# One decoder kernel: the seven-product up-projection with the queues of four engines in a hand-written order, and its gating moved from POOL to DVE

## The chip, the cores and the metric

The kernel runs on one core of a Trainium2 chip. A core has TensorE (PE, matrix products into the accumulators called PSUM), VectorE (DVE), ScalarE (ACT), GpSimd (POOL) and SyncE (SP, which here only issues DMA transfers). Each engine works through its own queue in order, and waits on semaphores that other engines raise. The metric is the device time of one execution in microseconds (us); the median of several runs is compared.

## What is computed

Two decoder layers over 512 tokens of width 1024 in float32. Each layer has a token mixer (dilated attention heads and mLSTM heads), a cross-attention into 256 memory tokens, and a gated MLP. The change touches the MLP:

```python
def conv_ffn(h, w_up, conv_w, conv_b, w_down):
    u = causal_dwconv(h @ w_up, conv_w, conv_b)      # width 3, along the tokens
    a, g = jnp.split(u, 2, axis=-1)                  # 2816 columns each
    return (jax.nn.gelu(g, approximate=True) * a) @ w_down
```

## The kernel before

Every float32 matrix product is made of three products of two-part operands. `split` makes the parts: ACT casts a tile to its high part (`hi`, line 99), then DVE subtracts that from the tile for the low part (`lo`, line 100). `mm3` then issues hi*hi, hi*lo and lo*hi (line 107).

The up-projection has 22 pairs of column blocks; pair j is one block of 128 linear columns (A) and one of 128 gate columns (G), against 512 tokens. Pairs 0 and 1 go through `feat_halves` as ordinary products. Pairs 2 to 21 go through `up_products`, the phase that the change rewrites. There a pair is taken as a 2 by 2 block product and is made with seven block products instead of eight (Winograd's form of Strassen's algorithm). One product is four `mm3`, so 12 matmuls of 256 columns, and a pair has 84 matmuls. There are 20 pairs in each of two layers, 40 in all.

For pair j the phase needs four kinds of weight operands, each split in high and low:

- `a`: the linear block as loaded (`raw`, line 86)
- `t` and `u`: sums made by POOL out of the two loaded blocks `raw` and `rg` (lines 1069 to 1072, four subtractions of 128x512: the first two make the tile `t12`, operand `t`; the last two make `t34`, operand `u`). Their tiles are named `T`
- `b`: one half of the gate block `rg`, loaded at line 1066

`raw` and `rg` have two buffers each. A buffer of `raw` comes free when POOL's fourth subtraction and the split of that pair have read it; only then can SP issue the load of the pair after next into it. The tile `T` has three buffers.

After the products come the sums in PSUM (ACT copies at lines 1105, 1123 and 1133, DVE additions at lines 1125 and 1134), the convolution of each half (`up_conv`: one ACT pass at line 1022, two DVE passes at line 1024, which read the accumulator), the GELU of the gate half (ACT, line 1027), and the product of both halves (POOL, line 1041), which goes to `down`, the down-projection.

Only PE's queue follows the order in which the code is written. The order of the other four queues is made by a scheduler, with a cost model, from the dependencies. PE takes, for pair j: product 5 of j, product 6 of j, product 4 of j-1, product 1 of j+1, then products 2, 3 and 7 of j.

Of the kernel before, what the change touches and what calls it, by code (L numbers as in the profile page):

```python
# [38 lines left out]
def trunk_kernel(ctx: ExitStack, tc: tile.TileContext, x4, memt, w, gw, gains, mcw, fcw, gb,  # L39
# [970 lines left out]
    def ffn(l, xn, pend, forms):  # L1010
# [8 lines left out]
        def up_conv(j, half, acc):  # L1019
            m = 22 * half + j  # L1020
            u = fp.tile([128, 512], F32, tag=f"u{half}", name=nm("u"), bufs=2)
            ACT.activation(u, acc, AF.Identity, bias=fcw_t[:, m, 3:4], scale=fcw_t[:, m, 2:3])  # L1022
            for q in range(1, 3):
                DVE.scalar_tensor_tensor(u[:, q:], acc[:, :512 - q], fcw_t[:, m, 2 - q:3 - q], u[:, q:],  # L1024
                                         ALU.mult, ALU.add)
            if half:
                ACT.activation(u, u, AF.Gelu_apprx_tanh)
            us[j, half] = u
            if (j, 1 - half) not in us:
                return  # L1030
# [10 lines left out]
            POOL.tensor_tensor(gt, us.pop((j, 0)), us.pop((j, 1)), ALU.mult)  # L1041
            gtiles.append(gt)

# [6 lines left out]
        run(up_products(l, fp, xn, forms, range(2, NF), up_conv))  # L1050
        return es, fp, gtiles

    def up_products(l, fp, xn, forms, pairs, done):


# [4 lines left out]
        left = {1: quarter(0, 0), 2: quarter(1, 0), 4: quarter(1, 1)}  # L1060
        left.update({3: forms.part("s4"), 5: forms.part("s1"), 6: forms.part("s2"), 7: forms.part("s3")})

        def weights(j):
            ra = load_raw(l, U_UP + 2 * j)
            rg = fp.tile([128, 1024], F32, tag="rg", name=nm("rg"), bufs=2)
            SP.dma_start(rg, w[l, U_UP + 2 * j + 1])
            b11, b21, b12, b22 = ra[:, :512], ra[:, 512:], rg[:, :512], rg[:, 512:]
            t12, t34 = forms.flat(), forms.flat()
            POOL.tensor_tensor(t12[:, :512], b12, b11, ALU.subtract)  # L1069
            POOL.tensor_tensor(t12[:, 512:], b22, t12[:, :512], ALU.subtract)  # L1070
            POOL.tensor_tensor(t34[:, :512], b22, b12, ALU.subtract)
            POOL.tensor_tensor(t34[:, 512:], b21, t12[:, 512:], ALU.subtract)  # L1072
            wa = w_split(ra, HALF_OFF)
            wt = w_split(t12, HALF_OFF)
            wb = forms.pool.tile([128, 1120], F32R, tag="b", name=nm("b"))
            wb = wb[:, 96:608], wb[:, 608:1120]
            split(b22, *wb)
            wu = w_split(t34, HALF_OFF)
            return {1: (wa, 0), 2: (wa, 512), 5: (wt, 0), 6: (wt, 512), 3: (wb, 0), 7: (wu, 0), 4: (wu, 512)}

        def product(o, ws, i, start=False):
            (hi, lo), c0 = ws[i]
            for q in range(4):
                c = slice(c0 + 128 * q, c0 + 128 * q + 128)
                rh, rl = left[i](q)
# [4 lines left out]
        hv = (slice(0, 256), slice(256, 512))  # L1090
        sums = [pg() for _ in range(4)]
        ws = {}
        e1s = {}
# [195 lines left out]
```

## Time and profile before

| | us |
|---|---|
| median of 3 runs | 1632.68 |
| lowest, highest | 1632.03, 1633.22 |
| the profiled execution | 1629.01 |
| its span, first to last instruction | 1627.0 |
| PE busy | 1556.9 (96%) |
| DVE busy | 1108.0 (68%) |
| ACT busy | 889.4 (55%) |
| POOL busy | 403.9 (25%) |

Matmuls overlap each other in the records, so a busy PE is not a PE at its peak. POOL works almost only in two stretches, one in each layer: the seven-product phases, from about 463 to 712 us and from about 1260 to 1506 us. The granted PE clock is full over the whole span. A timeline row gives the start in us, the length in us, engine, line, operation, output and inputs, shapes, and in brackets how long the engine stood idle before it and what released it.

### The profile page before, as it was taken

The page shows a single profiled execution, that of the slowest core. Times are in us where ns is not written, and L with a number is a line of the kernel's source. Part 1 is how long each engine was busy: PE and PEld are TensorE (multiplying, and loading weights), DVE is VectorE, ACT ScalarE, POOL GpSimd, SP SyncE. Part 2 cuts the span into 40 slices and gives each one's busy share as a digit, 9 for nine tenths or more (in the row PEclk, how much of TensorE's full clock was granted, in tenths as well). Part 3 has the DMA queues.
Part 4 walks back from the last instruction along what each step waited for, and adds up shares of the span by engine and source line. Part 5 has one row for each costly group of instructions (what it writes and reads, how often), then busy time and mean ns, then how long its engine had stood idle before and what let it go on. Part 6 is the DMA issues. An engine that isn't in the chain of part 4 may idle for free. (4 is left out here: it accounts for less than half of the span.)

```text
span 1627.0 us, 24707 instructions
## 1 busy us (share of the span) xinstructions
PE 1556.9 (96%) x9480; PEld 1372.9 (84%) x9480; DVE 1108.0 (68%) x1804; ACT 889.4 (55%) x1578; POOL 403.9 (25%) x296
## 2 busy tenths in 40 slices
PE   7999999999999998989999999999999899898998
PEld 5788888988899888878887888889888899897886
DVE  5688565756798787773377885656658899799433
ACT  5677564544665555552257775645445556556321
POOL 0000210000156576710010002100001767675000
PEclk9999999999999999999999999999999999999999
DMA  5322344551332222233233222444412222232321
GB/s 175 121 91 75 101 142 147 174 172 46 101 129 79 104 80 104 95 113 116 91 98 105 84 85 91 149 149 156 142 39 81 66 103 91 92 115 87 111 92 64
DMA packets 55432, 173.15 MB, mean 106 GB/s; under 512 B 6801, under 2 KB 9617, under 8 KB 55314
## 3 DMA queue, kind: packets, MB, share of 16 engines
q1 hardware_dynamic: 55314, 171.57, 32.0%
q8 instruction: 74, 1.21, 0.3%
q14 instruction: 44, 0.36, 0.1%
HBM read 165.22 MB, written 6.33 MB: 105 GB/s over the span
## 5 line engine op out<-in xcount | busy, mean ns | idle before, releaser
L100 DVE TENSOR_TENSOR wlo<-raw,whi 128x1024 fp32r<-128x1024 f32 x228 | 291.4, 1279 | 224.2 <-ACT whi L99 221.4
L107 PE MATMUL pg<-B,whi 128*128 128x256 f32 (+1 forms) x1800 | 421.1, 327 | 11.1 <-DVE u L1024 5.9
L99 ACT CAST whi<-raw 128x1024 fp32r<-128x1024 f32 x228 | 239.2, 1050 | 228.1 <-PE pg L107 158.9
L107 PEld LDWEIGHTS pg<-B,whi 128*128 128x128 f32 x1800 | 291.0, 189 | 31.4 <-issue 6.9
L107 PE MATMUL pg<-whi,B 128*128 128x512 f32 x896 | 297.6, 398 | 0.0
L107 PE MATMUL pg<-B,wlo 128*128 128x256 f32 (+1 forms) x896 | 288.6, 322 | 0.0
L107 PE MATMUL pa<-S,whi 128*128 128x256 f32 x960 | 178.2, 286 | 35.7 <-ACT pg L1105 35.5
L226 POOL TENSOR_TENSOR sm<-sm,mhalf 128x1 f32<-128x1 f32 x56 | 34.4, 614 | 688.1 <-DVE sm L351 511.8
L107 PEld LDWEIGHTS pg<-whi,B 128*128 128x128 f32 x896 | 168.5, 188 | 35.1 <-DVE B L100 1.3
L107 PEld LDWEIGHTS pa<-S,whi 128*128 128x128 f32 x960 | 147.7, 189 | 42.3 <-ACT pg L1105 42.1
L107 PEld LDWEIGHTS pg<-B,wlo 128*128 128x128 f32 x896 | 168.8, 188 | 13.7
L107 PE MATMUL pg<-wlo,B 128*128 128x512 f32 x448 | 175.2, 391 | 0.6 <-DVE sm L244 0.6
L1024 DVE SCALAR_TENSOR_TENSOR u<-pg,fcw,u 128x510 f32<-128x510 f32 (+1 forms) x176 | 130.4, 746 | 39.8 <-ACT u L1022 37.0
L100 DVE TENSOR_TENSOR wlo<-T,whi 128x1024 fp32r<-128x1024 f32 x80 | 128.5, 1610 | 33.2 <-ACT whi L99 32.6
L107 PE MATMUL pa<-S,wlo 128*128 128x256 f32 x480 | 135.3, 282 | 0.0
L107 PE MATMUL pg<-whi,S 128*128 128x512 f32 x352 | 116.3, 390 | 3.0 <-DVE u L1024 3.0
L107 PE MATMUL pa<-whi,S 128*128 128x512 f32 x352 | 116.4, 390 | 0.0
L99 ACT CAST whi<-T 128x1024 fp32r<-128x1024 f32 x80 | 84.1, 1052 | 46.5 <-POOL T L1072 27.4
L1069 POOL TENSOR_TENSOR T<-rg,raw 128x512 f32<-128x512 f32 x40 | 71.4, 1785 | 146.5 <-DMA rg<-in_w_dram 114.1
L1022 ACT ACTIVATE u<-pg,fcw 128x512 f32<-128x512 f32 x88 | 68.0, 776 | 71.1 <-DVE pg L1134 71.1
L107 PEld LDWEIGHTS pg<-wlo,B 128*128 128x128 f32 x448 | 84.7, 189 | 15.8 <-DVE wlo L100 1.0
L107 PEld LDWEIGHTS pa<-S,wlo 128*128 128x128 f32 x480 | 90.7, 189 | 0.0
(249 smaller groups left out, 2916.7 us busy)
## 6 DMA issues: line engine op xcount, KB each, us to landing
raw<-in_w_dram SPq DMA_DIRECT2D x228, 512.0 KB, 3.5
rg<-in_w_dram SPq DMA_DIRECT2D x40, 512.0 KB, 4.3
gain<-in_gains_dram SPq DMA_DIRECT2D x11, 512.0 KB, 4.5
raw<-in_memt_dram SPq DMA_DIRECT2D x20, 256.0 KB, 3.0
tb<-tb_d SPq DMA_DIRECT2D x16, 256.0 KB, 3.6
x<-in_x_dram SPq DMA_DIRECT2D x8, 256.0 KB, 5.7
e<-nmu_d SPq DMA_DIRECT2D x8, 256.0 KB, 3.7
dv<-vf SPq DMA_DIRECT2D x8, 256.0 KB, 4.2
```

Of the source, the lines that this page charges most:

```text
L99: ACT.copy(hi, src)
L100: DVE.tensor_sub(lo, src, hi.bitcast(F32))
L107: PE.matmul(o, lhs, rhs, **kw)
L226: POOL.tensor_tensor(r, v, mhalf[:, :1], ALU.pow)
L1022: ACT.activation(u, acc, AF.Identity, bias=fcw_t[:, m, 3:4], scale=fcw_t[:, m, 2:3])
L1024: DVE.scalar_tensor_tensor(u[:, q:], acc[:, :512 - q], fcw_t[:, m, 2 - q:3 - q], u[:, q:], ALU.mult, ALU.add)
L1069: POOL.tensor_tensor(t12[:, :512], b12, b11, ALU.subtract)
```

## The change

In `up_products` the queues of ACT, DVE, POOL and SP now follow the written order too, and the helper functions are taken apart so that this order can be written: `split` becomes `high` (ACT) and `low` (DVE), the loads become `load_a` and `load_g`, POOL's sums `add_up`, and the convolution `conv_first` (ACT) and `conv_rest` (DVE). Product 4 of pair j-1 moves ahead of product 6 of pair j. The gating (`gated`) is a DVE multiplication, no longer a POOL one. In this phase GELU writes its result into the gate's own accumulator in PSUM, and the gating reads it there. The sums that finish pair p = j-1 are issued at the start of step j. Loads of `raw` stand four pairs ahead in the code, loads of `rg` two pairs ahead. Numbers of buffers are unchanged.

```diff
-            POOL.tensor_tensor(gt, us.pop((j, 0)), us.pop((j, 1)), ALU.mult)
+            DVE.tensor_mul(gt, lin, gate)
             gtiles.append(gt)
...
-        run(up_products(l, fp, xn, forms, range(2, NF), up_conv))
+        with tc.manual_schedule(engines={mybir.EngineType.Activation, mybir.EngineType.DVE, mybir.EngineType.Pool,
+                                         mybir.EngineType.SP}):
+            run(up_products(l, fp, xn, forms, us, conv_first, conv_rest, gated))
...
+        def load_a(j):
+            if j < NF:
+                raws[j] = load_raw(l, U_UP + 2 * j)
+        def load_g(j):
+            if j < NF:
+                rgs[j] = fp.tile([128, 1024], F32, tag="rg", name=nm("rg"), bufs=2)
+                SP.dma_start(rgs[j], w[l, U_UP + 2 * j + 1])
...
+        def add_up(j):
+            if j < NF:
...
+                POOL.tensor_tensor(t12[:, :512], b12, b11, ALU.subtract)
+                POOL.tensor_tensor(t12[:, 512:], b22, t12[:, :512], ALU.subtract)
+                POOL.tensor_tensor(t34[:, :512], b22, b12, ALU.subtract)
+                POOL.tensor_tensor(t34[:, 512:], b21, t12[:, 512:], ALU.subtract)
...
+        def high(j, kind):
...
+            ACT.copy(ws[j, kind][0], source(j, kind))
+        def low(j, kind):
+            if j < NF:
+                DVE.tensor_sub(ws[j, kind][1], source(j, kind), ws[j, kind][0].bitcast(F32))
...
+        for j in range(j0, NF + 1):
+            p, real = j - 1, j < NF
+            if p >= j0:
+                A, G = total(p)
+                ACT.copy(A[:, right], e1s[p])
+                DVE.tensor_add(G[:, right], e1s[p], p5s[p])
+            low(j, "b")
+            load_g(j + 2)
+            if p >= j0:
+                conv_first(p, 1, G)
+            if real:
+                e5 = pa()[:, left]
+                yield from product(e5, j, 5, True)
+                p5s[j] = forms.pool.tile([128, 256], F32, tag="p5", name=nm("p5"), bufs=2)
+                ACT.copy(p5s[j], e5)
+            if p >= j0:
+                conv_rest(p, 1, G)
+                yield from product(A[:, right], p, 4)
+            low(j, "u")
+            if p >= j0:
+                conv_first(p, 0, A)
+                ACT.activation(G, us.pop((p, 1)), AF.Gelu_apprx_tanh)
+                conv_rest(p, 0, A)
+            if real:
+                yield from product(e1s[j], j, 6)
+                DVE.tensor_add(total(j)[1][:, left], e1s[j], p5s[j])
+            high(j + 1, "t")
+            low(j + 1, "t")
+            if p >= j0:
+                gated(p, us.pop((p, 0)), G)
+            if j + 1 < NF:
                 yield from first(j + 1)
...
+            high(j + 2, "a")
+            low(j + 2, "a")
+            if j + 1 < NF:
+                ACT.copy(total(j + 1)[0][:, left], e1s[j + 1])
+            add_up(j + 2)
+            load_a(j + 4)
+            if real:
+                yield from product(total(j)[0][:, left], j, 2)
+                high(j + 1, "u")
+                yield from product(total(j)[1][:, left], j, 3)
+                high(j + 1, "b")
+                yield from product(e1s[j], j, 7)
```

The order of ACT's queue before, one pair in the middle of layer 0 (`whi` is a high part from `T` or `raw`, `b` the gate half's, `pg` the sums A and G, `pa` the accumulator of products 1, 6 and 7, `p` the kept product 5, `u` the convolution's result):

```order
L1105 COPY pg_4934<-pa_6050 128x256
L99 CAST b_5998<-rg_5982 128x512
L1133 COPY pg_4932<-pa_5923 128x256
L1022 ACTIVATE u_6102<-pg_4933,fcw_4652 128x512
L1123 COPY p_1203_6145<-pa_6132 128x256
L99 CAST whi_6121<-T_6111 128x1024
L1027 ACTIVATE u_6102<-u_6102 128x512
L99 CAST whi_6128<-T_6112 128x1024
L1022 ACTIVATE u_6172<-pg_4932,fcw_4652 128x512
L99 CAST whi_6244<-raw_6234 128x1024
```

ACT's queue now, the same stretch of the phase:

```order
L1112 CAST whi_6046<-T_5942 128x1024
L1112 CAST whi_6064<-raw_5820 128x1024
L1191 COPY pg_4936<-pa_6051 128x256
L1112 CAST whi_6089<-T_5943 128x1024
L1112 CAST b_6104<-rg_5866 128x512
L1160 COPY pg_4934<-pa_5924 128x256
L1022 ACTIVATE u_6123<-pg_4935,fcw_4652 128x512
L1170 COPY p_1201_6138<-pa_6125 128x256
L1022 ACTIVATE u_6155<-pg_4934,fcw_4652 128x512
L1177 ACTIVATE pg_4935<-u_6123 128x512
```

The same instructions are there; the cast of the second `T` (operand `u`) now stands directly ahead of the cast of `b` and the copy that finishes A, where it stood after GELU. DVE's queue before, in the same place (`wlo` is a low part):

```order
L1134 TENSOR_TENSOR pg_4933<-pa_5923,p_1187_6018 128x256
L1024 SCALAR_TENSOR_TENSOR u_6102<-pg_4933,fcw_4652,u_6102 128x511
L1024 SCALAR_TENSOR_TENSOR u_6102<-pg_4933,fcw_4652,u_6102 128x510
L1125 TENSOR_TENSOR pg_4935<-pa_6050,p_1203_6145 128x256
L100 TENSOR_TENSOR wlo_6122<-T_6111,whi_6121 128x1024
L100 TENSOR_TENSOR wlo_6129<-T_6112,whi_6128 128x1024
L1024 SCALAR_TENSOR_TENSOR u_6172<-pg_4932,fcw_4652,u_6172 128x511
L1024 SCALAR_TENSOR_TENSOR u_6172<-pg_4932,fcw_4652,u_6172 128x510
L100 TENSOR_TENSOR wlo_6245<-raw_6234,whi_6244 128x1024
L100 TENSOR_TENSOR b_6125<-rg_6109,b_6125 128x512
```

DVE's queue now:

```order
L1161 TENSOR_TENSOR pg_4935<-pa_5924,p_1185_6011 128x256
L1116 TENSOR_TENSOR b_6104<-rg_5866,b_6104 128x512
L1027 SCALAR_TENSOR_TENSOR u_6123<-pg_4935,fcw_4652,u_6123 128x511
L1027 SCALAR_TENSOR_TENSOR u_6123<-pg_4935,fcw_4652,u_6123 128x510
L1116 TENSOR_TENSOR wlo_6090<-T_5943,whi_6089 128x1024
L1027 SCALAR_TENSOR_TENSOR u_6155<-pg_4934,fcw_4652,u_6155 128x511
L1027 SCALAR_TENSOR_TENSOR u_6155<-pg_4934,fcw_4652,u_6155 128x510
L1181 TENSOR_TENSOR pg_4937<-pa_6051,p_1201_6138 128x256
L1116 TENSOR_TENSOR wlo_6174<-T_6069,whi_6173 128x1024
L1041 TENSOR_TENSOR B_5922<-u_6155,pg_4935 128x512
L1116 TENSOR_TENSOR wlo_6192<-raw_5948,whi_6191 128x1024
```

The low part of the second `T` moved between the two convolutions, the low part of `b` from the end to the second place, and the gating (line 1041) came in as the eleventh instruction. SP's queue before, loads of `raw` (line 86) and `rg` (line 1066) in the middle of the phase:

```order
L1066 DMA rg_5854<-in_w_dram 128x1024
L86 DMA raw_6107<-in_w_dram 128x1024
L1066 DMA rg_5982<-in_w_dram 128x1024
L86 DMA raw_6234<-in_w_dram 128x1024
L1066 DMA rg_6109<-in_w_dram 128x1024
```

SP's queue now (`raw_5820` and `rg_5994` are the blocks of one pair):

```order
L1087 DMA rg_5866<-in_w_dram 128x1024
L86 DMA raw_5948<-in_w_dram 128x1024
L1087 DMA rg_5994<-in_w_dram 128x1024
L86 DMA raw_6075<-in_w_dram 128x1024
L1087 DMA rg_6121<-in_w_dram 128x1024
```

In both, `raw` of the next pair stands ahead of `rg` of this pair, one by one.

## Rows read from the trace of the kernel before

**Rows 1.** Windows, layer 1's phase: length, busy PE, PEld, DVE, ACT, POOL, clock.
```profile
1276.00:1488.00 212.00, 193.35 (x1586) 189.68 (x1586) 182.19 (x187) 119.91 (x187) 153.07 (x92) 1.00 0.26 93
```
**Rows 2.** Timeline of PE, first matmuls of two products that follow each other.
```profile
696.45 0.41 PE L107 MATMUL pg<-B,whi 128*128 128x256 f32 x2
...
697.89 0.41 PE L107 MATMUL pg<-B,whi 128*128 128x256 f32 x2
```
**Rows 3.** Waits of the whole run: who, for whom, us in total, times, longest.
```profile
POOL T L1069 <- DMA rg<-in_w_dram: 114.1, 33, 5.4
...
PE pa L107 <- ACT pg L1105: 35.5, 29, 2.9
...
ACT whi L99 <- POOL T L1072: 27.4, 28, 2.8
```
**Rows 4.** Timeline of POOL, one pair of layer 1 and the next one's start.
```profile
1397.79 1.82 POOL L1069 TENSOR_TENSOR T<-rg,raw 128x512 f32<-128x512 f32 x1 [3.61 <-DMA rg<-in_w_dram]
1399.68 1.31 POOL L1070 TENSOR_TENSOR T<-rg,T 128x512 f32<-128x512 f32 x1
1400.94 1.32 POOL L1071 TENSOR_TENSOR T<-rg 128x512 f32<-128x512 f32 x1
1402.23 2.26 POOL L1072 TENSOR_TENSOR T<-raw,T 128x512 f32<-128x512 f32 x1
1404.45 1.32 POOL L1041 TENSOR_TENSOR B<-u,u 128x512 f32<-128x512 f32 x1
1409.38 1.81 POOL L1069 TENSOR_TENSOR T<-rg,raw 128x512 f32<-128x512 f32 x1 [3.61 <-DMA rg<-in_w_dram]
```
**Rows 5.** Timeline of SP's queue in the same pair.
```profile
1404.52 0.33 SPq L86 DMA_DIRECT2D raw<-in_w_dram  x1
1404.94 0.39 SPq L1066 DMA_DIRECT2D rg<-in_w_dram  x1
```
**Rows 6.** Timeline of POOL, first subtraction of pairs 2, 5, 21 (layer 0), 5, 21 (layer 1).
```profile
463.36 1.79 POOL L1069 TENSOR_TENSOR T<-rg,raw 128x512 f32<-128x512 f32 x1 [15.99 <-DVE T L304]
...
496.94 1.33 POOL L1069 TENSOR_TENSOR T<-rg,raw 128x512 f32<-128x512 f32 x1 [5.92 <-issue]
...
683.10 2.25 POOL L1069 TENSOR_TENSOR T<-rg,raw 128x512 f32<-128x512 f32 x1 [2.57 <-DMA rg<-in_w_dram]
...
1292.80 2.34 POOL L1069 TENSOR_TENSOR T<-rg,raw 128x512 f32<-128x512 f32 x1 [5.09 <-DMA rg<-in_w_dram]
...
1476.56 2.29 POOL L1069 TENSOR_TENSOR T<-rg,raw 128x512 f32<-128x512 f32 x1 [2.54 <-DMA rg<-in_w_dram]
```
**Rows 7.** Timeline of ACT in the same pair of layer 1.
```profile
1397.06 0.62 ACT L99 CAST b<-rg 128x512 fp32r<-128x512 f32 x1
1397.58 0.38 ACT L1133 COPY pg<-pa 128x256 f32<-128x256 f32 x1
1398.88 0.78 ACT L1022 ACTIVATE u<-pg,fcw 128x512 f32<-128x512 f32 x1 [0.92 <-DVE pg L1134]
...
1401.03 1.05 ACT L99 CAST whi<-T 128x1024 fp32r<-128x1024 f32 x1 [1.11 <-POOL T L1070]
...
1404.53 1.05 ACT L99 CAST whi<-T 128x1024 fp32r<-128x1024 f32 x1 [1.92 <-POOL T L1072]
```
**Rows 8.** Timeline of DVE in the same pair of layer 1.
```profile
1398.36 0.42 DVE L1134 TENSOR_TENSOR pg<-pa,p 128x256 f32<-128x256 f32 x1
1399.69 1.53 DVE L1024 SCALAR_TENSOR_TENSOR u<-pg,fcw,u 128x511 f32<-128x511 f32 x2 [0.91 <-ACT u L1022]
...
1402.11 1.24 DVE L100 TENSOR_TENSOR wlo<-T,whi 128x1024 fp32r<-128x1024 f32 x1 [0.55 <-ACT whi L99]
...
1409.34 0.68 DVE L100 TENSOR_TENSOR b<-rg,b 128x512 fp32r<-128x512 f32 x1
```
**Rows 9.** Groups by line, whole run: a DVE product of an accumulator and an SBUF tile.
```profile
L359 DVE TENSOR_TENSOR hg<-pg,gain 128x512 f32<-128x512 f32 x32 | 21.9, 683 | 0.0
```
**Rows 10.** Timeline of PE, the first matmul of the down-projection in layer 0.
```profile
705.79 0.40 PE L107 MATMUL pa<-whi,S 128*128 128x512 f32 x1
```

More of the change, by code (lines that the diff above doesn't have):

```diff
@@ L1017, in ffn, with conv_first, conv_rest @@
         us = {}
-        def up_conv(j, half, acc):
+        def conv_first(j, half, acc):
             m = 22 * half + j
-            u = fp.tile([128, 512], F32, tag=f"u{half}", name=nm("u"), bufs=2)
+            us[j, half] = u = fp.tile([128, 512], F32, tag=f"u{half}", name=nm("u"), bufs=2)
             ACT.activation(u, acc, AF.Identity, bias=fcw_t[:, m, 3:4], scale=fcw_t[:, m, 2:3])
+        def conv_rest(j, half, acc):
+            m, u = 22 * half + j, us[j, half]
             for q in range(1, 3):
@@ L1025, in up_conv, with gated @@
                                          ALU.mult, ALU.add)
[L1026 to L1030, printed above, removed]
+        def gated(j, lin, gate):
             if j < 16:
@@ L1040, in up_conv @@
                 gt = pp.tile([128, 512], F32, tag="xg", name=nm("gt"), bufs=PACE["xg"])
-            POOL.tensor_tensor(gt, us.pop((j, 0)), us.pop((j, 1)), ALU.mult)
+            DVE.tensor_mul(gt, lin, gate)
             gtiles.append(gt)
+        def up_conv(j, half, acc):
+            conv_first(j, half, acc)
+            conv_rest(j, half, acc)
+            u = us[j, half]
+            if half:
+                ACT.activation(u, u, AF.Gelu_apprx_tanh)
+            if (j, 1 - half) in us:
+                gated(j, us.pop((j, 0)), us.pop((j, 1)))
         def up_done(j, half):
@@ L1058, in quarter @@
             return lambda q: (xn[kh][:, q, c], xn[2 + kh][:, q, c])
[L1060 to L1079, printed above, removed]
@@ L1081, in product @@
-        def product(o, ws, i, start=False):
-            (hi, lo), c0 = ws[i]
+        act = {1: quarter(0, 0), 2: quarter(1, 0), 4: quarter(1, 1)}
+        act.update({3: forms.part("s4"), 5: forms.part("s1"), 6: forms.part("s2"), 7: forms.part("s3")})
+        left, right = slice(0, 256), slice(256, 512)
+        sums = [pg() for _ in range(4)]
+        raws, rgs, ts, ws, e1s, p5s = {}, {}, {}, {}, {}, {}
+        def load_a(j):
+            if j < NF:
+                raws[j] = load_raw(l, U_UP + 2 * j)
@@ L1088, in product @@
                     yield
[L1090 to L1093, printed above, removed]
-        def total(j):
-            i = 2 * (j % 2)
-            return sums[i], sums[i + 1]
         def first(j):
-            e1s[j] = pa()
-            if j - pairs[0] < 2:
+            e1s[j] = pa()[:, left]
+            if j < j0 + 2:
                 for o in total(j):
-                    mm(o, ws[j][1][0][0][:, :128], xn[0][:, 0, :], start=True, stop=True)
-            yield from product(e1s[j][:, hv[0]], ws[j], 1, True)
-            ACT.copy(total(j)[0][:, hv[0]], e1s[j][:, hv[0]])
@@ L1136, in up_products @@
-        yield from last(pairs[-1])
+                    mm(o, ws[j, "a"][0][:, :128], xn[0][:, 0, :], start=True, stop=True)
+            yield from product(e1s[j], j, 1, True)
+        for j in (j0, j0 + 1):
+            load_a(j)
+            load_g(j)
+        add_up(j0)
+        load_a(j0 + 2)
+        for kind in "atu":
+            high(j0, kind)
+            if kind != "u":
+                low(j0, kind)
+        high(j0, "b")
+        yield from first(j0)
+        ACT.copy(total(j0)[0][:, left], e1s[j0])
```

57 lines of the change are left out of this document (28 added, 29 removed).

## The prediction

> **What bounds the kernel now.** I read four views, in this order: engine by stage, then PE's own spacing, then who waits for whom, then the timeline of the engine at the start of that chain. The change touches only the seven-product phase. There POOL, idle elsewhere, is busy 153.07 of 212 us and PE 193.35 [rows 1]: neither is full. One product takes PE 697.89 − 696.45 = 1.44 us [rows 2], so a pair cannot go below 7 × 1.44 = 10.08 us. What it takes is read from POOL, which starts one set of four subtractions per pair: 16 sets from pair 5 to pair 21 last 683.10 − 496.94 = 186.16 us in layer 0, or 11.635 each, and 1476.56 − 1292.80 = 183.76 in layer 1, or 11.485 [rows 6]. The mean is 11.56, so 1.48 us a pair is lost somewhere.
>
> The waits say where. PE waits 35.5 us for ACT, ACT waits 27.4 us for POOL, and POOL waits 114.1 us for the load of `rg` [rows 3]. The last looks like mere slack of a little-used engine, but the timeline shows a loop in it. POOL's fourth subtraction ends at 1402.23 + 2.26 = 1404.49 [rows 4]. It is the last reader of a `raw` buffer, and SP issues the next `raw` load at 1404.52, then the `rg` load behind it at 1404.94 [rows 5]. That one lands and lets POOL start the next set at 1409.38 [rows 4], 4.89 us after the fourth subtraction ended. So a cycle is 4.89 us plus what four subtractions take; with four free ones of about 1.31 that would be some 10.1, the same as PE's floor. The loss is in subtractions that take longer: 1.82 and 2.26 in place of 1.31 [rows 4].
>
> Their cause stands in DVE's rows. DVE's low part of `t` began at 1402.11 and took 1.24; POOL's fourth subtraction, begun at 1402.23, ended 1404.49 − 1403.35 = 1.14 us after DVE's end. DVE's low part of `b` (0.68) began at 1409.34, POOL's first subtraction at 1409.38, and it took 1.81 [rows 4, 8]. Whoever starts first, even by 0.04 us, goes at its own speed, and the other waits. DVE instructions that read an accumulator did not do this: the addition of 0.42 ran at 1401.14 [rows 8] beside POOL's third subtraction, which took 1.32.
>
> The Trainium skill ("SBUF — State Buffer", Who interferes with whom) has this as a lock: DVE with two SBUF inputs and a POOL instruction that reads SBUF exclude each other for the whole instruction, the first to issue wins, and DVE with at most one SBUF input stays out. The rows agree (2.26 against 1.31).
>
> **The change, part by part.** *The gating.* POOL loses 1.32 us per pair [rows 4]. That instruction stands behind the fourth subtraction and inside the wait of 3.61 us for `rg`, off the loop; taking it away gives 0, and the wait grows to 4.89. It could matter only if the wait fell under 1.3 us. DVE gains an instruction with one accumulator and one SBUF tile: 0.683 us is the nearest row [rows 9]. With it DVE has per pair three low parts of 1.24, one of 0.68, two convolutions of 1.53, two additions of 0.42 and the gating: 3.72 + 0.68 + 3.06 + 0.84 + 0.68 = 8.98 us, under 10.08, so DVE's load alone is no bound.
>
> By the skill's page the accumulator makes the gating lock-free, and a POOL instruction that could be blocked is gone; read so, the change should end the blocking. The rows say that the other contenders, the four subtractions and the low parts, all stay. The time by that reading is the third rival below.
>
> *SP.* `raw` of the next pair still stands ahead of `rg` of this one, with two buffers each. The loop of 4.89 us stays; loads that are written earlier do not leave earlier. Price 0.
>
> *The hand-written order of ACT and DVE.* This decides which low part meets which subtraction, and so the cycle. I walk one cycle from the end of POOL's fourth subtraction (time 0), with the durations and hand-overs of one pair [rows 4, 7, 8]. (a) ACT's high part of `u` starts at 0.04 (1404.53 − 1404.49) and takes 1.05. The next instruction of ACT starts 0.10 before the end of one (1397.06 + 0.62 against 1397.58): `b` from 0.99 to 1.61, the copy that finishes A from 1.51 to 1.89. (b) DVE's addition that finishes G starts 0.03 later (1401.03 + 1.05 against 1402.11), 1.92 to 2.34; `conv_first` 0.10 later (1398.36 + 0.42 against 1398.88), 2.44 to 3.22. (c) `conv_rest`, 1.53, from 3.25; DVE's next starts about 0.08 before its end (1399.69 + 1.53 against 1401.14). So the low part of `u` starts at 4.70, 1.24 long. (d) POOL's first subtraction starts at 4.89, 0.19 later: it is blocked and ends at 5.94 + 1.14 = 7.08. The second one starts 0.07 on (1399.61 against 1399.68) and ends at 8.46. (e) ACT's high part of `t` runs from 8.50 to 9.55, DVE's low part from 9.58 to 10.82. POOL's fourth subtraction would start 1.24 after the second's end (1400.99 against 1402.23), at 9.70: 0.12 too late, as in the rows of before, and ends at 10.82 + 1.14 = **11.96**. Should POOL win at (d), its first subtraction ends at 6.20, the waiting low part goes next, and the second ends at 6.20 + 1.24 + 1.14 = 8.58 in place of 8.46: cycle 12.08. So two long blocks per cycle either way. In the pair of before one of the two [rows 4] was the short one, behind `b`; the low part of `u` came at 1405.61 [rows 8], while POOL did work off the loop.
>
> Sum: 16 × (11.96 − 11.635) = 5.2 in layer 0 and 16 × (11.96 − 11.485) = 7.6 in layer 1. The first three cycles took 496.94 − 463.36 = 33.58 [rows 6]; with 3 × 11.96 = 35.88 each layer loses 2.3, so 4.6 (bounds 0 and, with a cycle twice disturbed, 9). After the last set the down-projection's first matmul came at 705.79 − 683.10 = 22.69 [rows 6, 10]. Now: 11.96 − 4.89 = 7.07 to the set's end, 1.89 until A's copy, then the last products; six without a wait are 8.64, which gives 17.6 at least. But product 6's addition stands behind the low part of `u`, as above, and the same chain repeats, so I take 22.69 unchanged (0; bounds −5 and +2 a layer).
>
> *PE's order.* Product 4 ahead of product 6 costs PE nothing by itself. It now waits for A's copy (1.89) directly; within a cycle of 11.96 against 10.08 that wait of nearly 2 us is a consequence, not an addition. *GELU into the accumulator* lies on ACT, which is busy 119.91 of 212 [rows 1] and idle then: 0; if it held up product 1's copy, some tenths per pair. *Pairs 0 and 1* are gated on DVE out of SBUF, four instructions of some 0.68 [rows 8] in a stretch where PE has plain products: 0, at most 2.7.
>
> Total +17.4: 1629.01 + 17.4 = 1646.4 for a profiled execution, which lies 3.67 under the median, so **1650** as a median.
>
> **The rivals.** *First, faster: one block per cycle.* If DVE's low part of `t` at (e) comes more than 0.12 us later, because ACT or DVE is still held by work that I put earlier, POOL's fourth subtraction starts first and ends at 9.70 + 1.29 = 10.99. Then the cycle is 10.99 to 11.1, the low part of `t` is late for product 5, which has slack. 32 × (11.05 − 11.56) = −16.3, the starts +2 to +4.6: about 1620 (1612 to 1632). For it: the margin is a tenth of a microsecond. Against it: both engines are idle ahead of this point in my walk, as they were in the rows of before (waits of 1.11 and 0.55), and there DVE won.
>
> *Second: the pace stays.* The scheduler's queues already hold these instructions at nearly these distances; if the new order settles in the same mix of collisions (`b` now at one subtraction, then at another), the cycle stays near 11.56 and only the starts count: 1633 to 1638. For it: the blocks of before wander too, 1.33 to 2.34 on the first subtraction alone [rows 6]. Against it: the low part of `b` has moved away from it.
>
> *Third: no block at all*, which is what the skill's lock-free gating would promise. Cycle 4.89 + 5.2 = 10.1, PE's floor: 32 × (10.1 − 11.56) = −46.7, about 1588. Against it: the low parts of `u` and `t` must run in the 4.89 us of POOL's wait, and `t` cannot, since it exists only after the second subtraction.
>
> *Fourth: slower still.* If A's copy or the low part of `u` is late for PE on top of the loop, the cycle exceeds 12.1; at 12.3, 1661.
>
> **How the numbers follow.** Forecast with its own range, 1638 to 1658: 0.56. Slower still: 0.08. First rival 0.21, second 0.10, third 0.05. Slower by over 0.2% (3.3 us, about what a measurement of this kernel can tell from no change) takes the forecast, the fourth and a little of the second: 0.66. Same: most of the second and the end of the first, 0.10. Faster: 0.24. A range of 8 in 10 reaches from the first rival's upper half, 1619, to 1661.
>
> **What would show it.** Right: sets about 12.0 apart; first subtraction near 2.2 us, second and third near 1.3, fourth near 2.26; DVE's low part of `u` starting within 0.3 us ahead of the first; SP's `raw` issued 0.03 after the fourth ends and `rg` 0.42 later; PE waiting nearly 2 us per pair for A's copy. Wrong: a fourth subtraction of 1.3 us (the first rival), an `rg` load that leaves well ahead of the fourth subtraction's end (then the loop that I rest on is not there), or PE products 1.44 us apart throughout (the third).

## The result, and the profile after

The changed kernel takes 1651.47 us in the median (1648.92 to 1655.14), the kernel before 1632.95. The ratio is 1.0114, with a 95% interval of 1.0092 to 1.0137: slower by about 1.1%. 1650 was forecast, slower.

| | before | after |
|---|---|---|
| median, us | 1632.95 | 1651.47 |
| the profiled execution, us | 1629.01 | 1655.14 |
| its span, us | 1627.0 | 1653.3 |
| POOL busy, us | 403.9 | 333.6 |
| DVE busy, us | 1108.0 | 1086.2 |

The profiled execution of after is the slowest of its four and that of before lies under all four of its runs, so the account below adds up to 26 us of span, where the medians differ by 18.5.

First the waits of the whole run (who waits for whom, us in total, times, longest us), which answer to [rows 3]:

```profile
POOL T L1093 <- DMA rg<-in_w_dram: 136.2, 26, 9.1
...
PE pg L107 <- ACT pg L1160: 53.2, 35, 2.5
```

POOL's wait for `rg` grew from 114.1 to 136.2 us: the 1.32 us of gating that left POOL went into it (3.61 in the pair of [rows 4], 4.93 in the one below). PE's wait of 53.2 us is for line 1160, the copy that finishes A, for which product 4 waits. The 35.5 us of [rows 3] were for another copy (line 1105, which takes product 1 out of its accumulator), so the two are not one wait that grew.

Then POOL, the timeline of one pair in layer 1 and the next set's start, which answers to [rows 4]:

```profile
1404.10 1.92 POOL L1093 TENSOR_TENSOR T<-rg,raw 128x512 f32<-128x512 f32 x1 [5.10 <-DMA rg<-in_w_dram]
1406.10 1.31 POOL L1094 TENSOR_TENSOR T<-rg,T 128x512 f32<-128x512 f32 x1
1407.36 1.31 POOL L1095 TENSOR_TENSOR T<-rg 128x512 f32<-128x512 f32 x1
1408.63 2.28 POOL L1096 TENSOR_TENSOR T<-raw,T 128x512 f32<-128x512 f32 x1
1415.84 2.09 POOL L1093 TENSOR_TENSOR T<-rg,raw 128x512 f32<-128x512 f32 x1 [4.93 <-DMA rg<-in_w_dram]
...
1420.54 2.29 POOL L1096 TENSOR_TENSOR T<-raw,T 128x512 f32<-128x512 f32 x1
```

SP in the same stretch, which answers to [rows 5]:

```profile
1410.94 0.33 SPq L86 DMA_DIRECT2D raw<-in_w_dram  x1
1411.37 0.37 SPq L1087 DMA_DIRECT2D rg<-in_w_dram  x1
```

The fourth subtraction ends at 1408.63 + 2.28 = 1410.91, `raw` leaves at 1410.94, `rg` at 1411.37, and the next set starts at 1415.84: the loop is there, 4.93 us of it outside POOL (4.89 before). The first and fourth subtractions are both stretched, the second and third are not.

The same holds over all 16 cycles of each layer, from the set of pair 5 to that of pair 21. The time from a set's end to the next set's start did not change: 5.24 and 5.00 us in the mean before (layers 0 and 1), 5.29 and 5.00 now. The set itself grew, from 6.40 and 6.48 us to 6.75 and 6.93, and that is nearly all of the change of the cycle. In pairs 6 to 21 the fourth subtraction is stretched (over 1.7 us) in all 32 sets, where it was in 12; the first in 29, where it was in 16.

DVE in the same pair, which answers to [rows 8]:

```profile
1412.81 0.43 DVE L1161 TENSOR_TENSOR pg<-pa,p 128x256 f32<-128x256 f32 x1 [0.82 <-ACT pg L1160]
...
1414.10 1.53 DVE L1027 SCALAR_TENSOR_TENSOR u<-pg,fcw,u 128x511 f32<-128x511 f32 x2 [0.26 <-ACT u L1022]
1415.55 1.22 DVE L1116 TENSOR_TENSOR wlo<-T,whi 128x1024 fp32r<-128x1024 f32 x1
...
1420.42 1.25 DVE L1116 TENSOR_TENSOR wlo<-T,whi 128x1024 fp32r<-128x1024 f32 x1 [1.88 <-ACT whi L1112]
1421.59 0.67 DVE L1041 TENSOR_TENSOR B<-u,pg 128x512 f32<-128x512 f32 x1
```

The low part of `u` starts at 1415.55, 0.29 us ahead of POOL's first subtraction; the low part of `t` at 1420.42, and POOL's fourth at 1420.54 takes 2.29. The gating from the accumulator (line 1041) takes 0.67. DVE gained some 30 us of gating and is still 22 us less busy, since it loses less to POOL: by the groups of instructions a low part of `b` takes 684 ns in the mean where it took 1407, one of `t` or `u` 1296 where it took 1610. In the new order POOL is more often the one that waits.

Last, the ends of the regular stretch, first subtraction of pairs 2, 5, 21 in layer 0 and of pairs 2, 5, 21 in layer 1, which answer to [rows 6]:

```profile
464.31 2.68 POOL L1093 TENSOR_TENSOR T<-rg,raw 128x512 f32<-128x512 f32 x1 [14.95 <-DVE B L273]
...
501.59 1.35 POOL L1093 TENSOR_TENSOR T<-rg,raw 128x512 f32<-128x512 f32 x1 [5.05 <-DMA rg<-in_w_dram]
...
694.38 1.31 POOL L1093 TENSOR_TENSOR T<-rg,raw 128x512 f32<-128x512 f32 x1 [6.07 <-DVE wlo L1116]
...
1270.89 1.64 POOL L1093 TENSOR_TENSOR T<-rg,raw 128x512 f32<-128x512 f32 x1 [8.71 <-DVE S L100]
...
1308.52 2.25 POOL L1093 TENSOR_TENSOR T<-rg,raw 128x512 f32<-128x512 f32 x1 [5.81 <-DVE u L1027]
...
1499.40 1.89 POOL L1093 TENSOR_TENSOR T<-rg,raw 128x512 f32<-128x512 f32 x1 [5.12 <-DMA rg<-in_w_dram]
```

From pair 5 to pair 21 there are 16 cycles: (694.38 − 501.59) / 16 = 12.05 us in layer 0, where it was 11.635, and (1499.40 − 1308.52) / 16 = 11.93 in layer 1, where it was 11.485 [rows 6]. From pair 21 of layer 0 to pair 5 of layer 1 it takes 614.14 us, where it took 609.70; the difference lies in the first three cycles of layer 1 (below).

### The profile page after: what moved, and what is told of

Its sections match the earlier page's. It is cut to its first block, busy times and chain, and to the rows that moved or that the text cites. A ratio compares the mean times of both kernels' runs of the same rounds, so it can differ in the third digit from the quotient of the medians.

```text
span 1653.3 us, 24516 instructions
## 1 busy us (share of the span) xinstructions
PE 1568.8 (95%) x9480; PEld 1382.6 (84%) x9480; DVE 1086.2 (66%) x1848; ACT 891.8 (54%) x1578; POOL 333.6 (20%) x252
## 4 chain that ended last, share of the span: by engine, by line
PE 56%; POOL 14%; DMA 13%; DVE 8%; issue 5%; ACT 4%; SPq 1%; POOLq 0%; DVEq 0%; ACTq 0%
PE pg L107 38%; PE pa L107 15%; DMA rg<-in_w_dram 8%; POOL T L1096 5%; POOL T L1093 4%; POOL T L1094 3%; DMA raw<-in_w_dram 2%; PE pa L111 2%; DVE wlo L100 2%; DVE u L1027 2%; DMA raw<-in_memt_dram 1%; POOL T L1095 1%; ACT whi L99 1%; DVE xg L252 1%; POOL sm L226 1%
## 5 line engine op out<-in xcount | busy, mean ns | idle before, releaser
L107 PE MATMUL pg<-B,whi 128*128 128x256 f32 (+1 forms) x1800 | 425.2, 329 | 60.3 <-ACT pg L1160 53.2
L100 DVE TENSOR_TENSOR wlo<-raw,whi 128x1024 fp32r<-128x1024 f32 x188 | 231.5, 1233 | 232.6 <-ACT whi L99 232.2
L99 ACT CAST whi<-raw 128x1024 fp32r<-128x1024 f32 x188 | 197.2, 1050 | 243.3 <-PE pg L107 163.9
L1116 DVE TENSOR_TENSOR wlo<-T,whi 128x1024 fp32r<-128x1024 f32 x80 | 103.7, 1296 | 63.2 <-ACT whi L1112 63.2
L1027 DVE SCALAR_TENSOR_TENSOR u<-pg,fcw,u 128x511 f32<-128x511 f32 (+1 forms) x176 | 131.0, 747 | 14.1 <-ACT u L1022 11.1
L1093 POOL TENSOR_TENSOR T<-rg,raw 128x512 f32<-128x512 f32 x40 | 75.3, 1883 | 218.4 <-DMA rg<-in_w_dram 136.2
L1096 POOL TENSOR_TENSOR T<-raw,T 128x512 f32<-128x512 f32 x40 | 87.2, 2180 | 0.0
```

The costliest lines, as they stand in the source:

```text
L99: ACT.copy(hi, src)
L100: DVE.tensor_sub(lo, src, hi.bitcast(F32))
L107: PE.matmul(o, lhs, rhs, **kw)
L1116: DVE.tensor_sub(ws[j, kind][1], source(j, kind), ws[j, kind][0].bitcast(F32))
```

## The experiments

Theory A is the prediction's: the loop (fourth subtraction, `raw` load, `rg` load, first subtraction) sets the pace, and a low part on DVE that starts just ahead of a subtraction stretches it. The rivals: B, PE's wait for the copy that finishes A is itself the bound; C, the order in which DVE feeds PE is; D, the move of the gating is. All ratios are to the kernel before, timed beside the run; there its median was 1628 to 1629 us, beside the changed kernel 1632.95. So a difference in us to 1651.47 holds to some 4 us, and the ratios are the better comparison.

| | edit to | us | ratio (95%) | cycle, layers 0 and 1 |
|---|---|---|---|---|
| before | | 1632.95 | 1 | 11.64, 11.48 |
| after | | 1651.47 | 1.0114 (1.0092 to 1.0137) | 12.05, 11.93 |
| e1_low_u | after | 1624.34 | 0.9962 (0.9947 to 0.9976) | 11.40, 11.26 |
| e2_pool_order | after | 1628.72 | 0.9993 (0.9979 to 1.0006) | 11.36, 11.19 |
| e3_both | after | 1598.58 | 0.9807 (0.9791 to 0.9824) | 10.54, 10.30 |
| e4_sp_order | after | 1594.38 | 0.9776 (0.9756 to 0.9796) | 10.39, 10.33 |
| e5_gate_pool | after | 1650.18 | 1.0122 (1.0096 to 1.0149) | 12.09, 11.94 |
| e6_before_gate_dve | before | 1654.16 | 1.0166 (1.0132 to 1.0201) | 12.41, 12.16 |
| e7_before_rg_first | before | 1610.50 | 0.9884 (0.9866 to 0.9902) | 10.91, 10.93 |
| e8_pe_order | after | 1652.91 | 1.0146 (1.0126 to 1.0166) | 12.00, 11.91 |
| e9_all_three | after | 1614.80 | 0.9918 (0.9895 to 0.9940) | 11.07, 11.01 |
| e10_sp_pool_order | after | 1597.91 | 0.9815 (0.9791 to 0.9839) | 10.50, 10.55 |

The cycle is the time between first subtractions, the mean over pairs 5 to 21, as above.

### Is it the low part of u that stretches the first subtraction?

```diff
             low(j, "b")
+            low(j, "u")
             load_g(j + 2)
...
                 yield from product(A[:, right], p, 4)
-            low(j, "u")
```

> One edit to the changed kernel: DVE's low part of u is written ahead of the gate half's convolution instead of behind it. Theory A (the loop fourth subtraction, raw load, rg load, first subtraction sets the pace, and a low part that meets a subtraction stretches it): in the changed kernel the low part of u starts 4.64 us after the fourth subtraction ends, 0.3 to 0.5 ahead of the first subtraction, which then takes about 2.05 us. Here it starts some 1.45 earlier and is over before the first subtraction starts, which falls to 1.31; the cycle falls from 11.93 by about 0.75 to 11.2, and 36 cycles give -27: 1624 us (1618 to 1632). Theory B (PE's wait for the copy that finishes A, 53.2 us in the changed kernel, is the bound by itself): the copy does not move, so 1651 within 4 us. Theory C (DVE's order of low parts and convolutions is what feeds PE): the convolution is 1.2 us later, 1655 or more.

Measured: 1624.34 us. POOL's timeline of one pair:

```profile
1406.64 1.31 POOL L1093 TENSOR_TENSOR T<-rg,raw 128x512 f32<-128x512 f32 x1 [4.94 <-DMA rg<-in_w_dram]
...
1410.58 2.26 POOL L1096 TENSOR_TENSOR T<-raw,T 128x512 f32<-128x512 f32 x1
```

and DVE's low part of `u` in it:

```profile
1404.54 1.22 DVE L1116 TENSOR_TENSOR wlo<-T,whi 128x1024 fp32r<-128x1024 f32 x1
```

The low part of `u` ends at 1405.76, ahead of 1406.64, and the first subtraction takes 1.31. The other stretched one stays as it was, and so does the loop (4.94). Nothing else was moved, and 27 us are gone, as A said. B and C fall, which gave 1651 and 1655 or more: the copy of A starts 1.50 us after the set's end in both kernels.

### And the low part of t the fourth?

```diff
                 POOL.tensor_tensor(t12[:, :512], b12, b11, ALU.subtract)
-                POOL.tensor_tensor(t12[:, 512:], b22, t12[:, :512], ALU.subtract)
                 POOL.tensor_tensor(t34[:, :512], b22, b12, ALU.subtract)
+                POOL.tensor_tensor(t12[:, 512:], b22, t12[:, :512], ALU.subtract)
                 POOL.tensor_tensor(t34[:, 512:], b21, t12[:, 512:], ALU.subtract)
```

> One edit to the changed kernel: POOL makes the first half of t34 (third subtraction) ahead of the second half of t12 (second subtraction), so that the last subtraction follows at once when t12 is done. Theory A: DVE's low part of t starts 1.12 us after t12 is complete. In the changed kernel the fourth subtraction starts 1.24 after it, so DVE wins and the fourth takes 2.28. Here the fourth starts at once and is nearly over when DVE comes: 1.31. t12 is complete 1.27 later, but nothing of the loop hangs on that. Cycle 11.93 - 0.95 = 11.0, 36 cycles, -34: 1618 us (1612 to 1628). Theory B (PE's wait for A's copy bounds by itself): t comes later and the copy no earlier: 1651 or a few us more. Theory C (the low part of t is what PE waits for): 1.27 later, slower, 1660 or more.

Measured: 1628.72 us, 23 under the changed kernel, 10 above what A said and just outside A's range (1612 to 1628). POOL in one pair:

```profile
1404.47 1.31 POOL L1093 TENSOR_TENSOR T<-rg,raw 128x512 f32<-128x512 f32 x1 [4.94 <-DMA rg<-in_w_dram]
1405.74 2.30 POOL L1094 TENSOR_TENSOR T<-rg 128x512 f32<-128x512 f32 x1
...
1409.36 1.30 POOL L1096 TENSOR_TENSOR T<-raw,T 128x512 f32<-128x512 f32 x1
```

and DVE's low parts of `t` (the pair before's), and of `u`:

```profile
1399.27 1.35 DVE L1116 TENSOR_TENSOR wlo<-T,whi 128x1024 fp32r<-128x1024 f32 x1 [1.76 <-ACT whi L1112]
...
1404.99 1.87 DVE L1116 TENSOR_TENSOR wlo<-T,whi 128x1024 fp32r<-128x1024 f32 x1
```

The fourth subtraction is free (1.30), as expected. But the low part of `t` now runs past the set's end (1399.54), the gating and the low part of `raw` follow it, and DVE comes to the low part of `u` later: at 1404.99, inside the first subtraction. It waits (1.87), goes in the gap between the first and the second subtraction, and the second takes 2.30. This is the branch of step (d) of the prediction in which POOL starts first, with the price that it gave: a stretched subtraction all the same, only another one. One was taken away and the other stayed; the expectation of 1618 had a cycle of 11.0, and it was 11.2 to 11.4.

### Both together

> The edits of e1_low_u and e2_pool_order together. Theory A: neither the first nor the fourth subtraction is stretched any more; a cycle is 4.93 + 4 x 1.27 = 10.0 to 10.2, PE's own 10.08 becomes the bound, and the wait of PE for A's copy goes with it: 36 x (10.25 - 11.93) = -60: 1591 us (1585 to 1603), faster than the kernel before. Theory B: no change, 1651. If the two stretched subtractions were one cost counted twice, about the better of the two single edits, 1618 to 1624.

Measured: 1598.58 us, inside A's range. No subtraction is stretched in the regular stretch (means of 1.29 to 1.32 over pairs 6 to 21 in layer 1), and the cycle is 10.30 there. POOL, one pair and the next one's start:

```profile
1402.45 1.30 POOL L1093 TENSOR_TENSOR T<-rg,raw 128x512 f32<-128x512 f32 x1 [5.04 <-DVE wlo L1116]
...
1406.37 1.29 POOL L1096 TENSOR_TENSOR T<-raw,T 128x512 f32<-128x512 f32 x1
1412.53 1.31 POOL L1093 TENSOR_TENSOR T<-rg,raw 128x512 f32<-128x512 f32 x1 [4.87 <-DMA rg<-in_w_dram]
```

The loop is still there (4.87); with four free subtractions it is as short as PE's floor of 10.08 us (1412.53 − 1402.45). This is the prediction's third rival, reached by moving the low parts out of the way rather than by the gating.

### Breaking the loop, and touching nothing else

```diff
             load_g(j + 2)
+            load_a(j + 3)
...
             add_up(j + 2)
-            load_a(j + 4)
```

(and the same for the one load ahead of the loop over pairs).

> One edit to the changed kernel: on SP the load of rg for a pair is issued ahead of the raw load that waits for the fourth subtraction, instead of behind it. Nothing moves on ACT, DVE or POOL. Theory A: rg then leaves as soon as its buffer is free (after the low part of b, some 9 us earlier), it is there when POOL wants it, and the loop is gone, though the low parts still meet the subtractions. The pace falls to PE's 10.08, with a remainder of tenths: 36 x (10.3 - 11.93) = -59: 1593 us (1586 to 1606). If the stretched subtractions alone set the pace and the loads do not: 1651, unchanged. Theory B (PE's wait for A's copy bounds by itself): 1651, unchanged.

Measured: 1594.38 us. DVE's low part of `b` and SP's load of `rg` in one pair:

```profile
1398.63 1.47 DVE L1116 TENSOR_TENSOR b<-rg,b 128x512 fp32r<-128x512 f32 x1
```

```profile
1400.16 0.33 SPq L1087 DMA_DIRECT2D rg<-in_w_dram  x1
```

POOL, with the end of one set and the next:

```profile
1399.51 1.74 POOL L1096 TENSOR_TENSOR T<-raw,T 128x512 f32<-128x512 f32 x1
1403.80 1.31 POOL L1093 TENSOR_TENSOR T<-rg,raw 128x512 f32<-128x512 f32 x1 [2.55 <-DMA rg<-in_w_dram]
1405.19 2.17 POOL L1094 TENSOR_TENSOR T<-rg,T 128x512 f32<-128x512 f32 x1
1407.31 2.29 POOL L1095 TENSOR_TENSOR T<-rg 128x512 f32<-128x512 f32 x1
1409.58 1.74 POOL L1096 TENSOR_TENSOR T<-raw,T 128x512 f32<-128x512 f32 x1
```

Here the subtractions are stretched more than in the changed kernel (1.31 + 2.17 + 2.29 + 1.74 = 7.51 against 1.92 + 1.31 + 1.31 + 2.28 = 6.82 in the set of after shown above), and the kernel is 57 us faster. `rg` leaves at 1400.16, when the low part of `b` has freed its buffer (1400.10) and ahead of the set's end (1401.25), so the next set starts 2.55 us after that end, not 4.93. The expectation was wrong in one point: `rg` leaves 1.1 us ahead of the set's end, where it left 0.5 behind it, not some 9 us earlier, and POOL still waits for it. The bound is elsewhere now: in the 130 us from 1290 to 1420 PE is busy for 130.00 and DVE for 129.12. So the stretched subtractions cost time only through the loop; the set's length alone is no bound. This run and e1 to e3 pull the two halves of A apart: shorten the set with the loop kept, or break the loop with the set longer.

### Is it the loop in the kernel before, too?

```diff
+        with tc.manual_schedule(engines={mybir.EngineType.SP}):
-        run(up_products(l, fp, xn, forms, range(2, NF), up_conv))
+            run(up_products(l, fp, xn, forms, range(2, NF), up_conv))
...
-            ra = load_raw(l, U_UP + 2 * j)
             rg = fp.tile([128, 1024], F32, tag="rg", name=nm("rg"), bufs=2)
             SP.dma_start(rg, w[l, U_UP + 2 * j + 1])
+            ra = load_raw(l, U_UP + 2 * j)
```

> The kernel before with the rg load written ahead of the raw load of its pair, and SP's queue alone kept in that written order in the phase, so that the rg load no longer stands behind the raw load that waits for the last fourth subtraction. ACT, DVE and POOL are still ordered by the scheduler. Theory A says that the loop paced the kernel before too: cycle 11.56 falls to between 10.3 and 11.1, 36 x (10.8 - 11.56) = -27: 1604 us (1590 to 1615). If the loop only arose in the hand-written order, no change: 1630.

Measured: 1610.50 us, faster than the kernel before by 1.2%. DVE's low part of `b`, SP's load of `rg`, then POOL at the end of one set and the next one's start (line numbers are one higher in this kernel from the loads on):

```profile
1405.86 1.79 DVE L100 TENSOR_TENSOR b<-rg,b 128x512 fp32r<-128x512 f32 x1
```

```profile
1407.72 0.33 SPq L1066 DMA_DIRECT2D rg<-in_w_dram  x1
```

```profile
1407.19 1.61 POOL L1073 TENSOR_TENSOR T<-raw,T 128x512 f32<-128x512 f32 x1
...
1412.85 1.66 POOL L1070 TENSOR_TENSOR T<-rg,raw 128x512 f32<-128x512 f32 x1 [2.77 <-DMA raw<-in_w_dram]
```

The set ends at 1408.80 and the next starts 4.05 later, with the load of `raw` now last. POOL's fourth subtraction no longer releases these loads: DVE's low part of `b` (to 1407.65) lets `rg` go at 1407.72, and `raw` follows at 1408.14, both ahead of the set's end. Loads that wait on DVE's work still pace the sets, so the loop is made shorter here rather than broken. The cycle falls from 11.56 to 10.92 although the set grew from 6.44 to 6.93 us in the mean; the time between sets fell from 5.12 to 3.99. The scheduler also made a new order (POOL's third subtraction now goes ahead of the second), so this run does not move the loads alone, but its gain lies between the sets, where A has it. The scheduler's order had the same loop; what it did not have was both long blocks in every cycle.

### The gating, moved alone in either direction

In the changed kernel, gating back on POOL, GELU back in SBUF:

```diff
-            DVE.tensor_mul(gt, lin, gate)
+            POOL.tensor_tensor(gt, lin, gate, ALU.mult)
...
-                ACT.activation(G, us.pop((p, 1)), AF.Gelu_apprx_tanh)
+                ACT.activation(us[p, 1], us[p, 1], AF.Gelu_apprx_tanh)
...
             load_a(j + 4)
+            if p >= j0:
+                gated(p, us.pop((p, 0)), us.pop((p, 1)))
```

> The changed kernel with the gating put back on POOL, behind the fourth subtraction of the next set, and with GELU writing into SBUF again; all other queues as in the changed kernel. Theory A (loop and stretched subtractions): POOL waits 4.93 us there, so 1.32 us of gating fit in without cost; DVE's two low parts that meet the subtractions stand where they stood, so about the time of the changed kernel, 1651 minus at most a few tenths per pair where DVE's 0.67 was ahead of something: 1648 (1634 to 1655). Theory D (the move of the gating to DVE is what made the kernel slower): back to 1630 or below.

Measured: 1650.18 us, the changed kernel's time. POOL around it:

```profile
1415.60 2.25 POOL L1041 TENSOR_TENSOR B<-u,u 128x512 f32<-128x512 f32 x1
1420.64 2.08 POOL L1093 TENSOR_TENSOR T<-rg,raw 128x512 f32<-128x512 f32 x1 [2.78 <-DMA rg<-in_w_dram]
```

Even stretched to 2.25 us the gating leaves 2.78 us of POOL's wait for `rg`: it is done long before the load lands. D falls; the gating lies off the loop on either engine.

In the kernel before, the one line that makes the product on DVE (`DVE.tensor_mul` of the two tiles in SBUF in place of `POOL.tensor_tensor`):

> The kernel before with one line changed: the gating product is a DVE instruction (two SBUF inputs, 0.68 us) in place of a POOL one; the scheduler sets all queues again. Theory A: POOL's gating lay off the loop, so nothing is gained, and DVE's added instruction shifts low parts against subtractions: between 1630 and 1662, by whether a cycle then holds one or two stretched subtractions (11.5 to 12.1 each). Theory D, in the sense that a POOL with less work is faster: under 1625.

Measured: 1654.16 us, within A's wide range; its cycles (12.41 and 12.16) are a little over the 11.5 to 12.1 that A gave. One set on POOL:

```profile
1413.41 1.31 POOL L1069 TENSOR_TENSOR T<-rg,raw 128x512 f32<-128x512 f32 x1 [4.92 <-DMA rg<-in_w_dram]
...
1416.41 2.28 POOL L1070 TENSOR_TENSOR T<-rg,T 128x512 f32<-128x512 f32 x1
```

The loop's 4.92 is unchanged; three subtractions of four are stretched, the longest to 2.28. The scheduler set all queues anew here, so this run does not price the gating itself; it shows that a new order by the same scheduler can meet as many low parts as the one by hand.

### PE's order

```diff
                 conv_rest(p, 1, G)
-                yield from product(A[:, right], p, 4)
...
+            if real:
+                yield from product(e1s[j], j, 6)
             if p >= j0:
+                yield from product(A[:, right], p, 4)
...
             if real:
-                yield from product(e1s[j], j, 6)
                 DVE.tensor_add(total(j)[1][:, left], e1s[j], p5s[j])
```

> The changed kernel with PE's order of before: product 4 of the last pair again behind product 6; the other queues keep the order of the changed kernel. Theory A: PE has nearly 2 us to spare in a cycle of 11.93, and the loop does not contain PE: 1651 within 3. Theory B (product 4 ahead of product 6, waiting for A's copy, holds PE up): 53 to 60 us of PE's waits on that copy shrink, and the time falls by 10 us or more, to 1640 or less.

Measured: 1652.91 us, no gain; its ratio lies 0.3 points above the changed kernel's, and the intervals overlap. The waits of the whole run:

```profile
PE pg L107 <- DVE pg L1182: 45.3, 32, 4.8
...
PEld pg L107 <- ACT pg L1160: 13.6, 32, 1.3
```

PE's wait for the copy of A (53.2 us) is gone from its matmuls (13.6 are left with the weight loads), and in its place stands one of 45.3 us for the addition behind product 6. PE has about 1.9 us per cycle to lose, and loses it wherever its queue first meets something late. B falls for good.

### All edits at once

> The edits of e1_low_u, e2_pool_order and e4_sp_order together in the changed kernel. If the loop's end and the unstretched subtractions add up, or PE's floor of 10.08 simply holds: 1588 to 1596, no worse than e4_sp_order. The other way: without the loop POOL starts a set as soon as a buffer of T is free, so the sets meet other low parts than before, and the one that starts second can now be DVE. In e4_sp_order DVE pays already: the low part of t takes 1.82, that of raw 1.73, that of b 1.47 in place of 1.24, 1.24 and 0.68, and its cycle of 10.1 holds no idle time any more. If the two edits that were made for the old meeting points make one more low part wait, by 0.9 us, DVE is the bound at 10.7 to 11: 1610 us (1604 to 1618).

Measured: 1614.80 us: three edits, of which two together gave 1598.58 and the third alone 1594.38, are 20 us slower than the third alone. The second alternative holds. DVE, the low parts of one whole cycle:

```profile
1415.34 1.23 DVE L1116 TENSOR_TENSOR wlo<-T,whi 128x1024 fp32r<-128x1024 f32 x1
...
1417.08 2.03 DVE L1116 TENSOR_TENSOR wlo<-raw,whi 128x1024 fp32r<-128x1024 f32 x1
...
1419.38 1.45 DVE L1116 TENSOR_TENSOR b<-rg,b 128x512 fp32r<-128x512 f32 x1
1420.75 2.31 DVE L1116 TENSOR_TENSOR wlo<-T,whi 128x1024 fp32r<-128x1024 f32 x1
...
1426.20 1.23 DVE L1116 TENSOR_TENSOR wlo<-T,whi 128x1024 fp32r<-128x1024 f32 x1
```

POOL's fourth subtraction in it, and the busy times of PE, PEld and DVE (the first three after the length) from 1290 to 1420 us:

```profile
1420.36 1.62 POOL L1096 TENSOR_TENSOR T<-raw,T 128x512 f32<-128x512 f32 x1
```

```profile
1290.00:1420.00 130.00, 122.73 (x1009) 120.26 (x1009) 129.15 (x133) 77.40 (x121) 77.57 (x49) 1.00 0.30 98
```

No instruction of that cycle has idle time ahead of it, those left out included: DVE is full, and its cycle is 1426.20 − 1415.34 = 10.86 us. Three low parts are stretched, that of `raw` to 2.03, of `b` to 1.45, of `u` to 2.31. POOL starts first there (its fourth subtraction 0.39 us ahead of the low part of `u`), and DVE pays. In e4_sp_order DVE was full as well (129.12 us of the same 130; its stretches stand in the expectation above), but PE was too (130.00, here 122.73): its cycle in that stretch was just PE's floor.

> The edits of e2_pool_order and e4_sp_order together. With the loop gone the order of the subtractions decides only which of the two engines waits: if DVE gets no more waits than in e4_sp_order, PE's floor holds, 1594 (1588 to 1600); if POOL's uninterrupted last two subtractions make DVE wait 0.5 us more per pair, 1612.

Measured: 1597.91 us, the first alternative; the cycle is 10.50 and 10.55, a little over e4_sp_order's. So the early low part of `u` is what costs in e9_all_three, since that run is this one and that edit. The lowest median is that of e4_sp_order, 0.9776 of the kernel before (0.9756 to 0.9796); e3_both and e10_sp_pool_order lie within 0.4 points of it, and the intervals overlap.

## Why the prediction was right, and where its sizes were off

- **The bound.** The loop was read from a wait that looked like slack. The totals of [rows 3] on the way to it are not one chain: in the same view of the kernel before, ACT's copy of line 1105 waits 58.6 us for DVE's convolution, not for POOL. But the loop itself rests on the timelines, and it held: 4.89 us outside POOL in the kernel before, 4.93 in the changed one, and breaking it alone gained 1651.47 − 1594.38 = 57 us in the changed kernel (3.4 points of the ratio; e4_sp_order). In the kernel before, taking the fourth subtraction out of it gained 1.2%, some 19 us, with a new order by the scheduler mixed in (e7_before_rg_first).
- **The walk of one cycle.** Against the fourth subtraction's end at 1410.91, DVE's addition that finishes G starts at 1.90 (1.92 forecast), the convolution at 3.19 (3.25), the low part of `u` at 4.64 (4.70), the first subtraction at 4.93 (4.89). The fourth subtraction takes 2.28 (2.26), and DVE's low part of `t` is 0.12 ahead of it in both. The cycle came out at 12.05 and 11.93, forecast 11.96.
- **Two sizes that cancel.** In most pairs `rg` lands a little later than in the one pair that I had (5.10 and 4.93 us of idle time in the two rows above, where 4.89 stood), and the first subtraction is shorter by as much (1.9 to 2.1 where 2.19 stood). That the two cancel is no luck: the first subtraction ends when the low part of `u` lets it, as step (d) has it. From the fourth's end to the first's end it is 7.00 to 7.03 us in 28 of the 32 cycles (7.08 in the walk), although `rg` lets the first start anywhere from 4.84 to 5.29. So in the changed kernel two paths run side by side there, the loads and the work on ACT and DVE up to the low part of `u`, and the second is the longer; that spread of the loads changes nothing.
- **The signs.** Two were off in size: the low part of `u` starts 0.2 to 0.7 us ahead of the first subtraction (within 0.3 stood), and PE's 35 waits for A's copy are 1.5 us long in the mean (nearly 2 stood).
- **The sum.** Layer 0: 192.79 − 186.16 = 6.6 (5.2 forecast); layer 1: 190.88 − 183.76 = 7.1 (7.6). The first three cycles: 37.28 − 33.58 = 3.7 in layer 0, and 37.63 − 33.15 = 4.5 in layer 1, where 2.3 each stood. That term was mis-sized, since I priced the first cycles like regular ones. SP, DVE and POOL at the start of layer 0's phase show one place where they differ:

```profile
475.77 9.08 SPq L86 DMA_DIRECT2D raw<-in_w_dram  x2
485.68 0.33 SPq L1087 DMA_DIRECT2D rg<-in_w_dram  x1
```

```profile
484.96 0.69 DVE L1116 TENSOR_TENSOR b<-rg,b 128x512 fp32r<-128x512 f32 x1
```

```profile
490.00 1.31 POOL L1093 TENSOR_TENSOR T<-rg,raw 128x512 f32<-128x512 f32 x1 [9.09 <-DMA rg<-in_w_dram]
```

The third set starts 9.09 us after the second one's end, for want of `rg`. That load leaves at 485.68, just after DVE's low part of `b` ends (485.65) and frees the buffer. In the written order this low part stands behind the gating of pairs 0 and 1 and a low part of `raw`; in the kernel before, the same load left at 470.88. The `raw` loads, which stand ahead of it on SP and which I had priced at 0, had left by 484.85 and did not hold it: in e4_sp_order, where `rg` stands ahead of the second of them, it leaves at 485.67. Layer 1 is alike (1290.56 and 1290.59). The first two cycles take 25.69 us in layer 0 where they took 16.94; the third takes 11.59 where it took 16.64. The bound of 9 for both layers held. The phase's end, from the last set to the down-projection's first matmul, took 23.59 and 24.17 us where it took 22.69 and 22.70; I took 0 with a bound of +2. Together cycles and starts are some 22 us where 17.4 stood, and the whole profiled span grew by 26.3. That the median lies within 1.5 us of 1650 is in part luck: the sum was some 9 us short for the profiled execution, which this time lies 3.67 above the median and not below it.

- **Costs taken as 0.** The gating off POOL (e5_gate_pool: 1650.18 against 1651.47) and PE's order (e8_pe_order: 1652.91) are 0 within some 5 us. GELU into the accumulator was not tried alone; it is undone in e5_gate_pool together with the gating, at no difference.
- **The rivals.** The first (one block per cycle, because POOL's fourth subtraction wins) did not arise: DVE's low part of `t` was about 0.1 us ahead in all 32 cycles. Its price was about right, as e2_pool_order shows, where the fourth goes first: 11.2 to 11.4 a cycle where 11.0 to 11.1 stood, and 1628.72 us in the rival's range of 1612 to 1632. The other branch of step (d) came true there too: the low part that had to wait went next and stretched the second subtraction. The third, by which the Trainium skill's reading of a lock-free gating would end the blocking, did not come true: the gating did not block and was not blocked (0.67 us, beside POOL's fourth subtraction, in the rows above), and the four subtractions were blocked as before.
- The Trainium skill ("SBUF — State Buffer", Who interferes with whom) says of DVE with two SBUF inputs and POOL that whoever issues first holds out the other for the whole instruction. The traces agree on both sides: POOL's subtraction of 2.28 behind a low part that was 0.12 us ahead, and DVE's low part of 2.31 in e9_all_three behind POOL.

## What to carry to other kernels

A long wait of a little-used engine for a DMA is slack only if the DMA was issued early: look up what released the issue, and if it is that same engine's last instruction, the two make a loop that the pace cannot beat, and a stretch of that engine's work inside it costs time in every cycle. Moving work to another engine gains nothing if it lay in the wait; here a swap of two DMA issues gained 57 us. Look also what else runs beside the load: its landing counts only where it is the last to come. Once the loop is broken, edits that served its timing can cost, so measure combinations, and look which engine has no idle time left.

## What was not expected of the hardware

A DVE low part that waits for a running POOL instruction goes between it and POOL's next one, though the two follow each other without a gap in the records (1404.47 + 1.31 against 1405.74), so that POOL then waits in its turn: in e2_pool_order the low part began 0.52 us into the first subtraction and took 1.87, and POOL's second took 2.30. In e9_all_three POOL's fourth subtraction goes first, and DVE's low part of `u` takes 2.31.
